# Fourteen instead of ten of the FFN's pairs computed by seven products of halves

## The chip, the cores and the metric

The kernel runs on one core of a Trainium2 chip: TensorE (PE) multiplies matrices, with its weight loads shown apart as PEld; VectorE (DVE), ScalarE (ACT) and GpSimd (POOL) do the rest; SyncE (SP) issues most DMAs. The metric is the device time of one execution in microseconds; the median of three runs before the change is 1286.7 us (1284.71 to 1290.56).

## The reference

A decoder trunk of two layers on 512 tokens of width 1024, in float32. Layer 0 mixes tokens with an RG-LRU block, layer 1 with RWKV-7; behind each stands the same gated FFN with a short convolution, which the change concerns:

```python
D_MODEL = 1024; SEQ = 512; D_FF = 3 * D_MODEL; FFN_CONV = 3

def _conv_ffn(x, norm, w_up, conv_w, conv_b, w_down):
    h = _rmsnorm(x, norm)
    u = jnp.einsum('btd,df->btf', h, w_up)
    gate = _causal_dwconv(u[..., :D_FF], conv_w, conv_b)
    hid = jax.nn.gelu(gate, approximate=True) * u[..., D_FF:]
    return jnp.einsum('btf,fd->btd', hid, w_down)
```

## The kernel before

Precision. Every float32 operand is split into a hi part (rounded, by ScalarE) and a lo part (the rest, by VectorE), and a product is three matmuls: hi x hi, hi x lo, lo x hi (mm3, lines 47 to 54). Each matmul has its own weight load.

The FFN. The 3072 gate columns and the 3072 up columns are cut into twelve *pairs* of 256 gate and 256 up columns (n = 0 to 11). Two pairs and the part of the down projection that has become ready make one period: the loop at the end of ffn runs the products of two pairs, up to product 7 of the odd one, and then down, inside which the odd pair's products 3 and 4 are put after the first piece of the first 512 columns.

A *whole* pair (class Whole) has four products G0, U0, G1, U1: 256 columns of gate or up, the upper or lower 512 of the 1024 inner rows, all 512 tokens. Each is 24 matmuls of 128x512 into banks accG and accU of PSUM, and has one weight of 512 KB to load and split (lines 94 and 97).

A *halves* pair (class Halves) sees gate and up as two column blocks, the inner rows as two halves and the tokens as two halves, and computes the eight products of such 2x2 blocks by seven, in the manner of Strassen and Winograd. Each is 24 matmuls of 128x256, named by number; they run in the order 1, 5, 6, 2, 7 and then 3, 4. They write three banks: A (products 1, 6, 7, 4 one on top of the other), F (5, then 3 on top) and D (2). Between products on one bank what stands there is read: ScalarE copies bank A after 1, 6 and 7 into a tile s (line 769), and VectorE adds bank F to the copy made after 7 (line 775), so that product 4 has to wait for that copy and product 3 for that addition. The token-side operands (sums of the input's halves) are made once for each layer.

A halves pair's weights are sums of blocks. Five tiles of 512 KB are loaded on SP's queue (line 166); to two of them (for products 5 and 7) an accumulating DMA from POOL's queue adds a second block as it loads (line 168). Product 6's weight is product 1's plus product 5's (VectorE, line 741), product 3's is product 6's plus one more block (an accumulating DMA, line 752, after 6's split). All seven are split (lines 747 and 748).

What sets the order. The tile framework schedules each engine's instructions from the program's order and its own estimates; each engine then takes its list in order. Weights are made two products ahead (ahead), loads of a halves pair start at G0 of the whole pair before it. All raw, hi and lo weight tiles of the kernel share one ring of 21 buffers of 4 KB a partition ("b4"): a load waits until the buffer it gets has been read for the last time.

Of the kernel before, what the change touches and what calls it, by code (L numbers as in the profile page):

```python
# [28 lines left out]
WARM2 = 20  # L29
WARM = 14  # L30

HALVES = (3, 5, 7, 9, 11)

PARAMS = [
    [("lru_b_in", 16), ("lru_conv_w", 32), ("lru_conv_b", 8),
# [9 lines left out]
class Kernel:  # L45
# [54 lines left out]
    def plan_weights(self):  # L100
# [4 lines left out]
        def piece(w, r0, c0, k):  # L105
            return w[r0 : r0 + k * P, c0 : c0 + D // k].rearrange("(k p) c -> p k c", p=P)
# [9 lines left out]
        def ffn(l):  # L116
            up, dn = I["ffn_w_up"][l], I["ffn_w_down"][l]

            def gu(six):


                for n in range(2 * six, 2 * six + 2):
                    self.quads.append(len(plan))
                    a = lambda i, j: piece(up, j * 512, (1 - i) * DFF + n * 256, 4)
                    if n in HALVES:
                        for first, more in (((0, 0), None), ((1, 1), (1, 0)), ((0, 1), None), ((1, 0), (0, 0)), ((1, 1), None)):
# [461 lines left out]
    def ffn(self, l, xs, finish, after=None):  # L588
        nc, tc = self.nc, self.tc
        last = l == 1  # L590
        with tc.tile_pool(name=f"ffn{l}", bufs=1) as pool:
# [21 lines left out]
            def start(c):  # L613
                if c == 0:
                    norm.append(self.norm_end(rbs))
                    next(norm[0])
                elif c == 1:
                    next(norm[0])
                    if last:
                        self.push(by_tokens())  # L620
# [14 lines left out]
            def operands():  # L635
                n1, t2, t3, t4 = sums

                def parts(t, k, f):
                    nc.scalar.copy(t[:, 0, k], f)
                    nc.vector.tensor_tensor(t[:, 1, k], f, t[:, 0, k].bitcast(F32), ALU.subtract)  # L640

                stt = nc.vector.scalar_tensor_tensor
                minus = pool.tile([P, 4], F32, name="minus")
                nc.vector.tensor_scalar(minus, self.vec("ffn_norm", l * 8 + 4, 4), -1.0, None, ALU.mult)
                for k in range(4):
                    x1, x2 = self.x[:, k, :], self.x[:, 4 + k, :]
                    d, f = two(t("s", 7)), two(t("s", 7))
                    nc.scalar.mul(d[:, 0], x1[:, H:], gain(k))
                    stt(d[:, 1], x1[:, 0:H], gain(k), d[:, 0], ALU.mult, ALU.subtract)
                    parts(n1, k, d[:, 1])  # L650
                    stt(f[:, 0], x2[:, H:], minus[:, k : k + 1], d[:, 1], ALU.mult, ALU.subtract)
                    parts(t2, k, f[:, 0])
                    stt(f[:, 1], x2[:, 0:H], minus[:, k : k + 1], f[:, 0], ALU.mult, ALU.subtract)
                    parts(t4, k, f[:, 1])
                    stt(d[:, 1], x2[:, H:], gain(4 + k), d[:, 0], ALU.mult, ALU.subtract)
                    parts(t3, k, d[:, 1])
                op = {i: [tuple(part[:, h] for part in xs[k + k0][:2]) for k in range(4)]
                      for i, k0, h in ((1, 0, slice(0, H)), (2, 4, slice(0, H)), (3, 4, slice(H, T)))}
                for i, v in ((5, n1), (6, t2), (7, t3), (4, t4)):
                    op[i] = [(v[:, 0, k], v[:, 1, k]) for k in range(4)]  # L660
                return op
# [133 lines left out]
            pairs, hids = {}, []  # L795
            kind = lambda n: Halves if n in HALVES else Whole
            seq = [(n, p) for n in range(12) for part in kind(n).order for p in part]
            made, at = [0], [0]

            def ahead(j):  # L800
                while made[0] < min(j, len(seq)):
                    n, p = seq[made[0]]
                    if n not in pairs:
                        pairs[n] = kind(n)(n)
                    pairs[n].weights(p)
                    made[0] += 1

            def products(upto, more=2):

                while True:  # L810
                    n, p = seq[at[0]]
                    at[0] += 1
                    ahead(at[0] + more)
                    pairs[n].product(p)
                    if p == "G0" and n + 1 in HALVES:
                        self.weights_load(quads[n + 1] + 4)
                    if n == 0 and p in ("G0", "U0"):
                        start(int(p == "U0"))
                    if n == 1 and p == "U0":
                        op.update(operands())  # L820
                    if p == 7:
                        self.weights_split(behind[n] + 2)
                    if (n, p) == upto:
                        return
# [57 lines left out]
            for n in range(3, 12, 2):  # L882
                products((n, 7))
                if n == 11 and not last:
                    self.norm_begin()
                    self.push(self.lora_weights())
                down(n, 2 * n - 6, 4 if n < 11 else 8, lambda: products((n, 4)), lambda: ahead(at[0] + 2))
# [898 lines left out]
```

## Time and profile before

| what | us |
|---|---|
| median of three runs | 1286.7 |
| the profiled execution | 1286.57 |
| its span, from the first to the last instruction | 1284.5 |
| the first FFN's period with pairs 6 and 7, busy TensorE | 63.0 of 63.0 |
| the same of the second FFN | 63.1 of 63.1 |

Times within the trace count from the start of the span. A row of a timeline gives start, duration, engine, line, operation, result and operands, and, in brackets, how long the engine had been idle before it and what released it. A group's row gives count and shortest, median and longest duration. For DMAs "to landing" is from issue to the data's arrival.

### The profile page before, as it was taken

Reading aid. Unit: us, or ns where it says so; the run is one execution under the profiler, and the core shown is the slowest. Engines: PE = TensorE matmul, PEld = TensorE weight load, DVE = VectorE, ACT = ScalarE, POOL = GpSimd, SP = SyncE. Lnnn points to the kernel's source line nnn. Section 1 sums busy time; section 2 is a strip of 40 time slices with the busy share of each in tenths; the row PEclk is TensorE's granted clock in tenths of the full one; section 3 lists DMA queues with packets and bytes.
Section 4 is the critical chain, followed back from the end, with each engine's and each line's share of the span. In section 5 each row is a group of like instructions: output and inputs, shape, how many; then the busy total and the mean of one; then the engine's idle time right before and its main releaser. Section 6 shows DMA issues by size and latency. Waiting matters only on the chain. (4 is left out here: it accounts for less than half of the span.)

```text
span 1284.5 us, 22413 instructions
## 1 busy us (share of the span) xinstructions
PE 1260.1 (98%) x9259; PEld 1069.9 (83%) x9259; DVE 928.6 (72%) x1412; ACT 643.5 (50%) x1006; POOL 134.1 (10%) x206
## 2 busy tenths in 40 slices
PE   9999999999999999999999999999999999999998
PEld 8777888989898989877678888778889898989896
DVE  5998678767676767788899867778866666666654
ACT  6697455434343343468745346545644343443442
POOL 3000001010100000010002144420010101000000
PEclk9999999999999999999799999999999999999999
DMA  7312335545454544422113122132355454545431
GB/s 220 113 52 97 98 120 111 164 99 177 86 180 83 180 96 122 148 66 79 66 48 92 52 62 81 48 100 77 110 110 163 100 177 86 181 82 181 95 136 65
DMA packets 117829, 141.37 MB, mean 110 GB/s; under 512 B 10138, under 2 KB 91748, under 8 KB 117600
## 3 DMA queue, kind: packets, MB, share of 16 engines
q1 hardware_dynamic: 100528, 122.44, 29.6%
q0 software_dynamic: 16624, 16.47, 8.3%
q8 instruction: 72, 1.18, 0.4%
q10 hardware_dynamic: 576, 1.05, 0.2%
q14 instruction: 29, 0.24, 0.1%
HBM read 135.41 MB, written 4.52 MB: 109 GB/s over the span
## 5 line engine op out<-in xcount | busy, mean ns | idle before, releaser
L97 DVE TENSOR_TENSOR wl<-raw,wh 128x1024 fp32r<-128x1024 f32 (+1 forms) x161 | 194.5, 1213 | 123.8 <-ACT wh L94 104.0
L94 ACT CAST wh<-raw 128x1024 fp32r<-128x1024 f32 (+1 forms) x161 | 166.0, 1043 | 181.6 <-PE acc L54 45.8
L54 PE MATMUL accU<-xs,wh 128*128 128x512 f32 x448 | 138.6, 391 | 0.0
L54 PE MATMUL accG<-xs,wh 128*128 128x512 f32 x448 | 138.6, 390 | 0.0
L54 PE MATMUL acc<-hid,wh 128*128 128x512 f32 x384 | 117.9, 389 | 0.0
L748 DVE TENSOR_TENSOR lo<-raw,hi 128x1024 fp32r<-128x1024 f32 x70 | 85.4, 1222 | 39.4 <-PE accU L54 32.0
L747 ACT CAST hi<-raw 128x1024 fp32r<-128x1024 f32 x70 | 73.6, 1053 | 60.4 <-PE accU L54 25.3
L54 PEld LDWEIGHTS accG<-xs,wh 128*128 128x128 f32 x448 | 83.7, 188 | 17.1
L54 PEld LDWEIGHTS accU<-xs,wh 128*128 128x128 f32 x448 | 83.6, 188 | 17.1
L54 PE MATMUL accU<-xs,wl 128*128 128x512 f32 x224 | 87.2, 389 | 0.0
L54 PE MATMUL accG<-xs,wl 128*128 128x512 f32 x224 | 87.2, 389 | 0.0
L54 PE MATMUL accA<-xt,hi 128*128 128x256 f32 x480 | 83.5, 277 | 0.0
L54 PEld LDWEIGHTS acc<-hid,wh 128*128 128x128 f32 x384 | 71.4, 188 | 14.3
L54 PE MATMUL acc<-xs,wh 128*128 128x512 f32 x256 | 80.9, 398 | 0.0
L694 DVE SCALAR_TENSOR_TENSOR cv<-gpad,pv,cv 128x512 f32<-128x512 f32 x96 | 69.1, 748 | 13.1 <-ACT cv L692 12.7
L848 PE MATMUL acc<-wh,hid 128*128 128x512 f32 (+1 forms) x200 | 76.2, 381 | 0.0
L849 PE MATMUL acc<-wl,hid 128*128 128x512 f32 (+1 forms) x200 | 76.1, 381 | 0.0
L847 PE MATMUL acc<-wh,hid 128*128 128x512 f32 (+1 forms) x200 | 76.1, 381 | 0.0
L168 POOL DMA_DIRECT2D raw<-in_ffn_w_up_dram x20 | 25.7, 1286 | 474.1 <-DVE x L863 166.2
L54 PE MATMUL acc<-hid,wl 128*128 128x512 f32 x192 | 74.3, 389 | 0.0
L54 PEld LDWEIGHTS accA<-xt,hi 128*128 128x128 f32 x480 | 72.6, 188 | 0.0
L54 PE MATMUL accA<-xt,lo 128*128 128x256 f32 x240 | 66.3, 276 | 0.0
(411 smaller groups left out, 2947.3 us busy)
## 6 DMA issues: line engine op xcount, KB each, us to landing
raw<-in_ffn_w_up_dram SPq DMA_DIRECT2D x106, 512.0 KB, 3.6
raw<-in_ffn_w_down_dram SPq DMA_DIRECT2D x48, 512.0 KB, 3.8
raw<-in_ffn_w_up_dram POOLq DMA_DIRECT2D x30, 512.0 KB, 5.7
raw<-in_rwkv_w_rkv_dram SPq DMA_DIRECT2D x24, 512.0 KB, 3.6
raw<-in_lru_w_in_dram SPq DMA_DIRECT2D x16, 512.0 KB, 4.0
raw<-in_lru_w_out_dram SPq DMA_DIRECT2D x8, 512.0 KB, 3.8
raw<-in_rwkv_w_out_dram SPq DMA_DIRECT2D x8, 512.0 KB, 3.4
xd<-x SPq DMA_DIRECT2D x8, 256.0 KB, 2.1
```

The source lines that it names most:

```text
L54: mm = lambda *a, **kw: self.nc.tensor.matmul(ps, *a, skip_group_check=more, **kw)
L94: put = (self.nc.vector.tensor_copy if dve else self.nc.scalar.copy)(hi, src)
L97: self.nc.vector.tensor_tensor(lo, src, hi.bitcast(F32), ALU.subtract)
L168: self.nc.gpsimd.dma_start(raw, more, accum_op=ALU.add)
L694: nc.vector.scalar_tensor_tensor(cv, pair.gp[:, e, j : j + T], cw(j), cv, ALU.mult, ALU.add)
L747: nc.scalar.copy(hi, f[p])
L748: tt(lo, f[p], hi.bitcast(F32), ALU.subtract)
L847: nc.tensor.matmul(ps, hh[:, s], wh[:, k, m], start=kk == 0, stop=False)
L848: nc.tensor.matmul(ps, hl[:, s], wh[:, k, m], start=False, stop=False)
L849: nc.tensor.matmul(ps, hh[:, s], wl[:, k, m], start=False, stop=kk == blocks - 1)
```

## The change

Pairs 6 and 10 join the list of those that are computed by halves; each period from n = 6, 7 and from n = 10, 11 then has two halves pairs in a row. The hooks are moved to fit: the loads of an odd halves pair behind an even halves pair are called for at product 6 of that even pair, and the next weights are split at product 7 of odd pairs only.

```diff
-HALVES = (3, 5, 7, 9, 11)
+HALVES = (3, 5, 6, 7, 9, 10, 11)
...
                     pairs[n].product(p)
-                    if p == "G0" and n + 1 in HALVES:
+                    if p in ("G0", 6) and n % 2 == 0 and n + 1 in HALVES:
                         self.weights_load(quads[n + 1] + 4)
...
-                    if p == 7:
+                    if p == 7 and n % 2:
                         self.weights_split(behind[n] + 2)
```

In the rows below, raw58 to raw62 are the loaded weights of pair 6, raw63 to raw67 those of pair 7 (in order of products 1, 5, 2, 7, 4); hi and lo carry the number of the product, accA_2934 and accF_2965 are banks of pair 6, accA_3178 is bank A of pair 7, wh and wl are the split weights of the down projection.

TensorE in the first FFN, before: the end of product 7 of pair 7, and the piece of the down projection that follows.

```order
L54 MATMUL accA_3082<-xt_1485,hi7_3140 128x256 x2
L54 MATMUL accA_3082<-xt_1485,lo7_3141 128x256
L54 MATMUL acc0_3245<-hid_2525,wh67_3235 128x512 x2
L54 MATMUL acc0_3245<-hid_2525,wl67_3236 128x512
L54 MATMUL acc0_3245<-hid_2525,wh67_3235 128x512 x2
```

And now, behind product 7 of pair 6: the last of the six matmuls of pair 7's product 1, nine of pair 6's product 4, and the first of its product 3.

```order
L54 MATMUL accA_3178<-xs1_1279,hi1_3095 128x256 x2
L54 MATMUL accA_3178<-xs1_1279,lo1_3096 128x256
L54 MATMUL accA_2934<-xt_1486,hi4_3063 128x256 x2
L54 MATMUL accA_2934<-xt_1486,lo4_3064 128x256
L54 MATMUL accA_2934<-xt_1486,hi4_3063 128x256 x2
L54 MATMUL accA_2934<-xt_1486,lo4_3064 128x256
L54 MATMUL accA_2934<-xt_1486,hi4_3063 128x256 x2
L54 MATMUL accA_2934<-xt_1486,lo4_3064 128x256
L54 MATMUL accF_2965<-xs4_1412,hi3_3032 128x256 x2
```

Where a piece of 24 down matmuls of 128x512 lay between products 7 and 4, there are six matmuls of 128x256 now.

ScalarE at the same place, before: its copies after products 1, 6 and 7 of pair 7, with casts of down weights between them.

```order
L769 COPY s_3107<-accA_3082 128x512
L747 CAST hi4_3201<-raw66_3138 128x1024
L769 COPY s_3168<-accA_3082 128x512
L94 CAST wh67_3235<-raw67_3233 128x1024
L94 CAST wh68_3241<-raw68_3239 128x1024
L769 COPY s_3229<-accA_3082 128x512
```

And now the copies of pair 6.

```order
L769 COPY s_2959<-accA_2934 128x512
L747 CAST hi3_3032<-raw58_2749 128x1024
L769 COPY s_3020<-accA_2934 128x512
L747 CAST hi4_3063<-raw62_2990 128x1024
L747 CAST hi1_3095<-raw63_3022 128x1024
L747 CAST hi5_3125<-raw64_3024 128x1024
L769 COPY s_3091<-accA_2934 128x512
```

The casts of pair 7's first two weights, of which raw64 is one that an accumulating DMA adds to, stand ahead of the copy after product 7.

VectorE at the end of pair 5, before: from the gate's rows to the first sum of the down projection.

```order
L782 SCALAR_TENSOR_TENSOR gpad1_1480<-accA_2554,rb_1565 128x2x256
L97 TENSOR_TENSOR wl59_2921<-raw59_2860,wh59_2920 128x1024
L694 SCALAR_TENSOR_TENSOR cv_2799<-gpad1_1480,pv_79,cv_2799 128x512
L694 SCALAR_TENSOR_TENSOR cv_2804<-gpad1_1480,pv_79,cv_2804 128x512
L694 SCALAR_TENSOR_TENSOR cv_2799<-gpad1_1480,pv_79,cv_2799 128x512
L694 SCALAR_TENSOR_TENSOR cv_2804<-gpad1_1480,pv_79,cv_2804 128x512
L863 TENSOR_TENSOR x_68<-x_68,acc0_2717 128x512
```

And now.

```order
L741 TENSOR_TENSOR raw58_2749<-raw59_2751,raw58_2749 128x1024
L748 TENSOR_TENSOR lo5_2790<-raw59_2751,hi5_2789 128x1024
L694 SCALAR_TENSOR_TENSOR cv_2819<-gpad1_1480,pv_79,cv_2819 128x512
L694 SCALAR_TENSOR_TENSOR cv_2824<-gpad1_1480,pv_79,cv_2824 128x512
L694 SCALAR_TENSOR_TENSOR cv_2819<-gpad1_1480,pv_79,cv_2819 128x512
L694 SCALAR_TENSOR_TENSOR cv_2824<-gpad1_1480,pv_79,cv_2824 128x512
L97 TENSOR_TENSOR wl56_2837<-raw56_2721,wh56_2836 128x1024
L863 TENSOR_TENSOR x_68<-x_68,acc0_2717 128x512
```

Pair 6's sum and split have come ahead of the convolution, and the lo part of the third down weight, which was made earlier, has come behind it. The lo part of the fourth (wl57) has moved behind the eight sums and products that follow.

## The prediction

> **What bounds the kernel now.** The page comes first, then the busy time by stretches of the second FFN, then the chain of waits there.
>
> ```profile
> span 1284.5 us, 22413 instructions
> PE 1260.1 (98%) x9259; PEld 1069.9 (83%) x9259; DVE 928.6 (72%) x1412; ACT 643.5 (50%) x1006; POOL 134.1 (10%) x206
> ...
> core 0: us, PE busy (x) PEld busy (x) DVE busy (x) ACT busy (x) POOL busy (x), PEclk, DMA share, GB/s
> 374.90:437.90 63.00, 63.00 (x361) 55.50 (x361) 41.70 (x51) 24.98 (x31) 3.81 (x3) 1.00 0.50 133
> 1066.90:1129.99 63.09, 63.09 (x362) 55.58 (x361) 39.87 (x48) 25.27 (x30) 3.85 (x3) 1.00 0.50 134
> ```
>
> A stretch of 63 us is one period: a whole pair, a halves pair and their share of the down projection, in layer 0 (first row) and layer 1 (second). TensorE is busy in all of it and the clock is 1.00, so only matmul time can be taken away there. VectorE has 41.7 of 63.0 us, ScalarE 25, the DMA engines half. The chain of one period in layer 1:
>
> ```profile
> 1066.90 5.44 PE accG L54 x24
> 1072.34 5.44 PE accU L54 x24
> 1077.78 5.44 PE accG L54 x24
> 1083.22 5.44 PE accU L54 x24
> 1088.66 2.87 PE accA L54 x24
> 1091.53 2.74 PE accF L54 x24
> 1094.27 2.72 PE accA L54 x24
> 1096.99 2.86 PE accD L54 x24
> 1099.85 2.74 PE accA L54 x24
> ...
> 1108.05 2.87 PE accF L54 x24
> 1110.92 2.74 PE accA L54 x24
> ...
> 1129.99 5.44 PE accG L54 x24
> ```
>
> The columns are start, duration, what. A whole pair is four products of 24 matmuls, 4 x 5.44 = 21.76 us. A halves pair is seven products (in order 1, 5, 6, 2, 7 and, after a piece of the down projection, 3 and 4): 2.87 + 2.74 + 2.72 + 2.86 + 2.74 + 2.87 + 2.74 = 19.54 us. The rest of the 63.09 is 21.79 us of down projection.
>
> **The change part by part.** Pairs 6 and 10 turn from whole to halves in both layers: four times 21.76 - 19.54 = 2.22 us of matmuls go, 8.9 us. Nothing more can be won: TensorE has no idle time in these stretches that could vanish too.
>
> At one place a rule of the Trainium skill speaks against this. TensorE: Matmul & The Clock Gate, section Back-to-back issue gap, says that in a stream of weight loads and matmuls the spacing is set by both, and gives 131 ns a matmul at 512 columns and 81 at 128. By those figures a whole pair's 96 matmuls would take 12.6 us and a halves pair's 168 at least 13.6, a loss. The trace disagrees: 24 matmuls of 512 columns take 5.44 us, 227 ns each, and 24 of 256 take 2.72 to 2.87, 113 to 120 each.
>
> What the other engines get, per changed pair:
>
> ```profile
> 376.76 2.73 DVE L694 SCALAR_TENSOR_TENSOR cv<-gpad,pv,cv 128x512 f32<-128x512 f32 x4
> 379.42 1.28 DVE L863 TENSOR_TENSOR x<-x,acc 128x512 f32<-128x512 f32 x2
> 380.61 1.29 DVE L787 TENSOR_TENSOR s<-s,ge 128x512 f32<-128x512 f32 x2
> 382.42 1.29 DVE L789 TENSOR_TENSOR hid<-s,hid 128x512 fp32r<-128x512 f32 x2
> 394.18 1.23 DVE L741 TENSOR_TENSOR raw<-raw,raw 128x1024 f32<-128x1024 f32 x1
> 402.08 2.55 DVE L748 TENSOR_TENSOR lo<-raw,hi 128x1024 fp32r<-128x1024 f32 x2 [3.20 <-PE accU L54]
> 364.58 0.69 DVE L775 TENSOR_TENSOR s<-s,accF 128x512 f32<-128x512 f32 x1 [0.46 <-ACT s L769]
> ```
>
> VectorE: a whole pair has four weight splits of 1.2 us, eight operations of 0.68 and the convolution's 2.7, some 13 us. A halves pair has seven splits and an addition (8 x 1.23 = 9.8), seven of 0.69 (4.8), the convolution (2.7) and lines 787 and 789 (2.6), 19.9 us. That is 7 us more: 48.6 of a period of 60.9, 80%. ScalarE goes from 25 to 30 us (three more casts of 1.05 us, three copies of 0.59). Both stay below TensorE, so their work costs nothing on average; what can cost is its place in a queue. DMA: eight transfers of 512 KB for four (five on SP's queue, three accumulating on POOL's), from 8.4 to 10.5 MB a period, a share of about 0.65.
>
> Three places have little room. I count from t = 0 at 374.9, when the last matmul of the halves pair before the changed one ends, with operations back to back on VectorE at the spacing of the rows (0.60 for 128x512, 0.66 for line 694, 1.13 for 128x1024).
>
> *First, the down weights.* TensorE does the second piece of the first down columns (24 x 0.227 = 5.4), then seven matmuls that need no lo part, and wants the third piece's lo at 7.0. VectorE has the gate (0.1 to 0.7), the new line 741 and the new split (to 3.0), the convolution (to 5.65), then that lo: ready at 6.9. The fourth lo is wanted at 13.2, after 25 more down matmuls and four of product 1; VectorE adds eight operations of 0.60 and has it at 12.8. So 0.1 and 0.4 us are left; I count 0.2 us of waiting, between 0 and 0.8 (half of one more 1.13 operation at each).
>
> *Second, and the main term, the accumulated weight of the next pair.* So far the 21.76 us of a whole pair lay between two halves pairs, time in which the next one's weights came in. Now pair 7's loads reuse buffers that pair 6 still reads: by the waits in the program, its first weight waits for the split of pair 6's product 7, its second (the one that a second DMA adds to) for the end of product 1. The other two loads stand behind these on SP's queue. Product 1 ends at 19.2 (all down matmuls 16.3 + 2.87); VectorE ends that split at about 19.0, so the second load goes out at 19.4, one of three in a row.
>
> ```profile
> 424.65 0.88 SPq L166 DMA_DIRECT2D raw<-in_ffn_w_down_dram  x2
> DMA to landing us min/median/max: 3.7/4.1/4.6
> ...
> DMA to landing us min/median/max: 3.6/4.1/5.2
> ...
> L168 POOL DMA_DIRECT2D raw<-in_ffn_w_up_dram x20: 1258/1276/1378, 195.1 to 1195.4; - x20
> ...
> DMA to landing us min/median/max: 5.6/5.7/7.6
> ```
>
> The first two lines are a burst of two loads of 512 KB (3.7 and 4.6), the third four loads within 6.6 us, the last the accumulating loads. So: 19.4 + 4.6 = 24.0, POOL issues the accumulation, + 5.7 = 29.8. (Behind it on POOL stands only the one for product 7 of pair 7, wanted 14 us later or more.) ScalarE takes its instructions in order, and the cast of this weight now stands ahead of the copy of bank A after pair 6's product 7:
>
> ```profile
> 391.36 1.05 ACT L747 CAST hi<-raw 128x1024 fp32r<-128x1024 f32 x1 [0.30 <-PE acc L54]
> 363.96 0.59 ACT L769 COPY s<-accA 128x512 f32<-128x512 f32 x1 [1.10 <-PE accA L54]
> ```
>
> Cast to 30.8, copy to 31.4, and TensorE goes on at 31.5. It had finished product 7 at 30.2 (19.2 + 2.74 + 2.72 + 2.86 + 2.74) and six matmuls of pair 7's product 1 at 31.0, and stands before product 4, which may not write bank A until the copy is done: 0.5 us of waiting. Each us that the accumulation is later is a us more; 1 us earlier and there is none. With the longest rows (5.2 and 7.6) it is 3.0. I take the likelier rows: 0.5.
>
> *Third*, product 3 wants line 775, which VectorE does after the new line 741 on the same weight: 741 ends at 31.4, 775 at 32.1, and product 3 begins at 31.5 + 1.0 (nine matmuls; fifteen in layer 1) = 32.5. It hides behind the second wait.
>
> The order is the same at pairs 6 and 10 of both layers, so each saves 2.22 - 0.7 = about 1.5: 6.1 us in all. The profiled execution took 1286.57 us (its span and 2.1 around it), the median is 1286.7: forecast 1286.6 - 6.1 = **1280.5 us**.
>
> **The rivals.** *All hidden.* With loads that land in 3.7 and 5.7 us the cast is over before the copy is due, and 1286.6 - 8.9 = 1277.7 follows. For it: the lengths are the common ones. Against: three loads leave in a row, and the first two waits leave 0.1 and 0.4 us.
>
> *The wait eats the saving.* Two us more at each place (accumulations beside other loads, as they now are): 2.7 us of waiting each, and 1286.6 + 4 x 0.5 = 1288.6. For it: the 7.6 in the row, 1.9 above the median. Against: that one is rare.
>
> *Slower.* One mechanism, the same chain (load, accumulation, cast, copy, product 4), beside twice as many accumulations: with the longest landing of a plain load in layer 1,
>
> ```profile
> DMA to landing us min/median/max: 3.3/3.7/6.8
> ```
>
> 6.8 and 7.6 give 2.2 + 1.9 more, 4.8 us a place: 1286.6 + 4 x 2.6 = 1297. It decides from a chain that is 1.5 us longer than I count.
>
> *Weight loads set the pace.*
>
> ```profile
> L54 PEld LDWEIGHTS accA<-xt,hi 128*128 128x128 f32 x480 | 72.6, 188 | 0.0
> ```
>
> If 188 ns a load could not overlap, a halves pair would take 168 x 0.188 = 31.6 us, 9.8 more than a whole one, and the time would be 1326; it decides from 21.76 / 168 = 130 ns a matmul. The halves pairs that run already show 113 to 120. The Trainium skill's rule above is this rival.
>
> **How the numbers follow.** All hidden (under 0.3 us a place) 0.25; the forecast (0.3 to 1.4) 0.47; the wait eats the saving (1.4 to 3.8) 0.20; slower 0.07; weight loads 0.01. A measurement of this kernel can tell about 0.5%, 6.4 us, from no change: faster means below 1280.3. All of the first case is there and 0.17 of the second, 0.42; slower is the last two, 0.08; within 0.5% has the other 0.50. The range, 1277.0 to 1288.6, goes from the first case less 0.7 of scatter to the third's price, and leaves out the slower cases and the longest waits of the third.
>
> **What would show it.** Right: a period of about 61.5 us with pair 6 or 10 in it, seven products of 2.7 to 2.9 us, and one short wait of TensorE before product 4 of the even pair, released by ScalarE's copy, with an accumulating load behind it. Wrong: periods of 60.9 with no gap (all hidden); gaps over 2.2 us (saving eaten); gaps at the lo parts of the down weights instead (VectorE short of time); products longer than 3 us; or a difference outside the FFN.

## The result, and the profile after

The changed kernel takes 1303.57 us (median of four runs, 1301.74 to 1307.06), the kernel before in the same comparison 1285.7 us (1283.18 to 1290.56): a ratio of 1.0147, 95% interval 1.0113 to 1.0182. It is slower by 1.5%, and the interval is clear of 1. The forecast was 1280.5 us with a range up to 1288.6.

The head of the page of after (the profiled execution took 1307.06 us):

```profile
span 1305.3 us, 23093 instructions
PE 1261.0 (97%) x9547; PEld 1081.4 (83%) x9547; DVE 952.7 (73%) x1440; ACT 658.4 (50%) x1030; POOL 149.2 (11%) x218
```

TensorE's busy time has not fallen by 8.9 us, and the span has grown by 20.8 us. The wait view of TensorE shows the first half of the reason (two FFNs, apart by the "..."; columns: us in total, times, longest):

```profile
PE accA L54 <- ACT s L769: 5.3, 2, 3.2
PE acc L54 <- ACT wh L94: 3.0, 2, 1.7
PE acc L54 <- DVE wl L97: 1.7, 2, 0.9
...
PE accA L54 <- ACT s L769: 6.6, 2, 3.4
PE acc L847 <- ACT wh L94: 3.7, 2, 1.9
PE acc L849 <- DVE wl L97: 0.9, 1, 0.9
```

Before, this view was empty in the stretches with pairs 6 to 11. Now there are 21.2 us: 9.3 at the down weights (the prediction's first place) and 11.9 at the copies of bank A (its second). The second half of the reason stands in stretches of 2 to 7 us around pairs 6 and 7 of layer 0 (columns as in the prediction; the clock, the DMA share and GB/s are the last three):

```profile
304.00:309.00 5.00, 5.00 (x34) 4.61 (x33) 0.00 (x0) 1.05 (x1) 0.00 (x0) 1.00 0.99 328
322.00:328.00 6.00, 6.00 (x30) 5.04 (x29) 6.00 (x10) 3.01 (x4) 0.00 (x0) 1.00 0.01 3
334.00:341.00 7.00, 7.00 (x63) 7.00 (x63) 1.22 (x1) 3.04 (x4) 0.42 (x1) 1.00 1.12 321
...
348.00:350.00 2.00, 2.00 (x11) 2.00 (x12) 2.00 (x3) 0.79 (x1) 0.00 (x0) 0.61 0.30 47
350.00:352.00 2.00, 2.00 (x12) 2.00 (x11) 1.44 (x2) 0.00 (x0) 0.26 (x1) 0.54 0.00 0
```

Two things are to be seen. The DMA engines are full at 304 to 309 and at 334 to 341 us and idle at 322 to 328 between: the loads come in bursts. And at 348 us the clock drops to about half for some 3.4 us. The chain of waits tells what happened there (start, duration, what):

```profile
301.34 7.51 DMA raw<-in_ffn_w_up_dram
...
309.41 5.91 DMA raw<-in_ffn_w_up_dram
...
334.37 5.67 DMA raw<-in_ffn_w_up_dram
...
340.57 5.67 DMA raw<-in_ffn_w_up_dram
...
347.90 1.89 PE accA L54 x9
349.79 3.83 PE accF L54 x24
```

The first two rows are the load and the accumulation of pair 6's second weight, the next two those of pair 7's. Where before the chain was TensorE alone, it now goes through these transfers. The last two rows are the slow clock: 9 matmuls in 1.89 us instead of 1.02, 24 in 3.83 instead of 2.87, 1.8 us together. The two FFNs have five such stretches: one behind each of the four waits for a copy and one behind the down weights' waits in layer 1. The queues in which the late weights stand, on ScalarE:

```profile
315.40 1.05 ACT L747 CAST hi<-raw 128x1024 fp32r<-128x1024 f32 x1 [6.88 <-DMA raw<-in_ffn_w_up_dram]
316.36 1.52 ACT L692 ACTIVATE cv<-gpad,pv 128x512 f32<-128x512 f32 x2
317.78 1.03 ACT L94 CAST wh<-raw 128x1024 fp32r<-128x1024 f32 x1
...
346.32 1.04 ACT L747 CAST hi<-raw 128x1024 fp32r<-128x1024 f32 x1 [2.92 <-DMA raw<-in_ffn_w_up_dram]
347.27 0.58 ACT L769 COPY s<-accA 128x512 f32<-128x512 f32 x1
```

and on VectorE:

```profile
315.42 1.23 DVE L741 TENSOR_TENSOR raw<-raw,raw 128x1024 f32<-128x1024 f32 x1 [2.66 <-DMA raw<-in_ffn_w_up_dram]
```

At the first place both engines stand before pair 6's second weight until 315.4, with the down weights' cast (line 94 at 317.78) behind it. At the second ScalarE stands 2.92 us before pair 7's second weight, with the copy behind it.

By stages: from its first G0 matmul to RWKV's first matmul, the first FFN went from 368.1 to 379.7 us; from there to the second FFN's first G0 matmul the RWKV stage went from 366.7 to 362.4; the second FFN, to the end, from 393.2 to 406.6. In the FFNs: 7.4 saved (by e5's periods, below), 21.2 of waits, 0.6 of waits for hid (the FFN's gated hidden rows) at the end of the first FFN, five times about 1.8 for the clock, 23.4 in all, of the 25.0 measured; 1.6 are not traced. Of the RWKV stage's 4.3 some 3.4 go with its clock, which was at half for 13.7 us in the profiled execution of before and for 6.8 in that of after; the change does not touch this stage. The profiled execution of after is the slowest of its four, with a mean granted clock of 0.989 against 0.991 to 0.992, so the count of five is that of this execution.

### The profile page after: what moved, and what is told of

Same layout as the page of the kernel before. It is cut to its first block, busy times and chain, and to the rows that moved or that the text cites. A ratio compares the mean times of both kernels' runs of the same rounds, so it can differ in the third digit from the quotient of the medians.

```text
span 1305.3 us, 23093 instructions
## 1 busy us (share of the span) xinstructions
PE 1261.0 (97%) x9547; PEld 1081.4 (83%) x9547; DVE 952.7 (73%) x1440; ACT 658.4 (50%) x1030; POOL 149.2 (11%) x218
## 4 chain that ended last, share of the span: by engine, by line
PE 71%; DVE 13%; DMA 8%; ACT 4%; issue 2%; POOL 0%; SPq 0%; POOLq 0%; ACTq 0%; DVEq 0%
PE acc L54 19%; PE accA L54 9%; PE accU L54 8%; PE accG L54 8%; DMA raw<-in_ffn_w_up_dram 8%; PE accF L54 5%; PE acc L849 3%; PE acc L847 3%; PE acc L848 3%; PE accD L54 2%; DVE wl L97 2%; DVE X L1309 1%; PE acc L1255 1%; DVE mt L970 1%; PE s L1423 1%
## 5 line engine op out<-in xcount | busy, mean ns | idle before, releaser
L747 ACT CAST hi<-raw 128x1024 fp32r<-128x1024 f32 x98 | 103.1, 1052 | 163.4 <-DMA raw<-in_ffn_w_up_dram 55.6
L748 DVE TENSOR_TENSOR lo<-raw,hi 128x1024 fp32r<-128x1024 f32 x98 | 119.0, 1221 | 49.8 <-PE accA L54 22.2
L54 PE MATMUL accA<-xt,hi 128*128 128x256 f32 x672 | 120.5, 282 | 11.9 <-ACT s L769 11.9
L54 PEld LDWEIGHTS accA<-xt,hi 128*128 128x128 f32 x672 | 103.9, 192 | 12.7 <-ACT s L769 12.7
L54 PE MATMUL accU<-xs,wh 128*128 128x512 f32 x320 | 99.2, 391 | 0.0
L54 PE MATMUL accG<-xs,wh 128*128 128x512 f32 x320 | 99.2, 391 | 0.0
L54 PE MATMUL accA<-xt,lo 128*128 128x256 f32 x336 | 94.4, 281 | 0.0
L54 PEld LDWEIGHTS accG<-xs,wh 128*128 128x128 f32 x320 | 59.6, 188 | 12.1
L54 PEld LDWEIGHTS accA<-xt,lo 128*128 128x128 f32 x336 | 64.7, 193 | 0.0
L54 PE MATMUL accU<-xs,wl 128*128 128x512 f32 x160 | 62.3, 390 | 0.0
```

Source lines behind the costliest of these rows:

```text
L54: mm = lambda *a, **kw: self.nc.tensor.matmul(ps, *a, skip_group_check=more, **kw)
L747: nc.scalar.copy(hi, f[p])
L748: tt(lo, f[p], hi.bitcast(F32), ALU.subtract)
```

## The experiments

The kernel before was run beside each. "Waits" are sums of TensorE's wait view over the two FFNs as above; the two-pair period runs from G0 of pair 4 to G0 of pair 8 and was 126.2 us before in both layers.

**Which accumulated weight.** e1, e2 and e5 leave out the accumulation to product 5's weight in pairs 7 and 11, in 6 and 10, or in all four. All matmuls, casts and additions of the engines are done, with incomplete weights.

```diff
-... ((1, 1), (1, 0)), ...
+... ((1, 1), None if n in (7, 11) else (1, 0)), ...
```

> Left out: the block that an accumulating DMA adds to the weight of product 5 of pairs 7 and 11 (2 DMAs a layer). Theory (the four waits before product 4 of pairs 6 and 10, 11.9 us, come from this accumulation, whose cast ScalarE has ahead of the copy of bank A; the half clock behind each of them, 3.4 us long and so 1.7 us, is their consequence): these waits fall below 1 us in all, the clock stays at 1.00 there, time 1303.6 - 11.9 - 4 x 1.7 = about 1285. Rival, VectorE is short of time (its work stays as it is): waits of the same sum in another place, time above 1297. Rival, the clock dips by itself (more weight loads, not the waits): only the 11.9 go, the four half-clock stretches stay, time about 1292.

> Left out: the block that an accumulating DMA adds to the weight of product 5 of pairs 6 and 10. Theory (at the border from pair 5 to 6 and from 9 to 10 ScalarE holds the cast of this weight ahead of the gate and of the down weights' casts, and VectorE the sum of line 741): the 8.8 us of waits for casts of down weights and the 4.6 us for their lo parts go to under 3 us in all, the waits before product 4 (11.9 us) stay: time about 1303.6 - 11 = 1292 to 1293. Rival, VectorE is short of time: at least half of the 13.4 us stays, time above 1297.

> Left out: the added block of product 5's weight in pairs 6, 7, 10 and 11, the two omissions of the first two experiments together. Theory (two waits at each place, independent of each other, both from an accumulating load ahead of other work in ScalarE's queue): the waits are gone, 8.9 us of matmuls are saved, time 1284.7 - 8.9 = 1276 to 1278. Rival (what is left of the waits, 8.5 us in the first experiment, is VectorE's lack of time and only moves): at least 5 us of waits in the FFNs, time 1281 or more.

e1: 1286.33 us, ratio 1.0014 (0.9999 to 1.0030); of the waits at the copies 1.4 us is left, those at the first place are 7.1 (9.3 in after), and there is no stretch of half clock in the FFNs. e2: 1288.99 us, 1.0043 (1.0026 to 1.0060); the down weights' waits are gone, the copies' are 11.4. e5: 1277.55 us, 0.9949 (0.9931 to 0.9967), periods of 124.33 us in both layers. TensorE's waits in e5 are no more than

```profile
PE acc L54 <- DVE hid L789: 0.4, 1, 0.4
PE acc L54 <- ACT hid L788: 0.2, 1, 0.2
...
PE accA L54 <- ACT s L769: 1.3, 1, 1.3
```

So most of the saving is there (1.9 us a period, where 2.22 were forecast), VectorE and ScalarE with all of their added work are not short of time, and with the accumulations the waits of both places go. Leaving out an accumulation also takes 512 KB out of a burst of transfers, so these three runs do not tell the late weight from the load on the DMA engines; the runs from e4 on leave nothing out. Without the one the kernel gains 17.2 us on after (e1), without the other 14.6 (e2), without both 26.0: the two gains overlap, though e5 expected them to be independent.

**One of the two pairs.** e3 takes pair 10 back out of the list: HALVES = (3, 5, 6, 7, 9, 11).

> Pair 6 by halves, pair 10 whole, in both layers (12 pairs of 24). Theory (a loss of the same size at each of the four places, 17.9 / 4 = 4.5 us): half of the loss, time 1285.7 + 9 = about 1294.7, two waits before product 4 instead of four. Rival, the time goes lost elsewhere (the end of a layer, the RWKV stage with another order): nearer to 1285.7 or to 1303.6 than to the middle.

1292.76 us, 1.0057 (1.0030 to 1.0084), with waits of 6.6 and 5.7 us, all at pairs 6 and 7. With one place in each layer instead of two, about 0.4 of after's loss (0.57 of 1.47 per cent) is left: the loss goes by places.

**The place in the queue.** e4 puts the copy of bank A ahead of the odd pair's cast, and line 775 ahead of its line 741:

```diff
+ with tc.issue_after(pairs[pair.n - 1].add.ins):      # pairs 7, 11
      tt(f[1], f[5], f[1], ALU.add)
...
+ with tc.issue_after(pairs[pair.n - 1].put.ins):      # product 5 of pairs 7, 11
      nc.scalar.copy(hi, f[p])
```

> All 14 pairs, nothing left out; only the order of two instructions on ScalarE and of two on VectorE: the cast of pair 7's (11's) second weight is held behind the copy of bank A after pair 6's (10's) product 7, the sum of line 741 behind line 775. Theory (it is the place in the queue that makes the late transfer cost TensorE's time): the 11.9 us before product 4 go, and the half clock behind them, time about 1285, though the transfers land as late as before. Rival, the transfers are too late in any order (TensorE then waits for pair 7's product 5 instead): waits of 8 us or more before products 5 or 6 of pairs 7 and 11, time above 1297.

1293.66 us, 1.0081 (1.0052 to 1.0110): half of the expected gain. The copies' waits fall from 11.9 to 4.9 and the clock stays full, but 7.9 us of waits are left at other places (0.6 of them for hid, as in after), and those for lo parts of down weights have grown from 2.6 us (three) to 6.0 (eight). What the late weight holds up moves down the queue. In e4's chain of waits the next late one is pair 7's last accumulated weight, that of product 3 (line 752, which is 756 in e4), for which ScalarE's next cast waits until 357.56. POOL's row of it, and the chain's:

```profile
351.24 1.27 POOL L756 DMA_DIRECT2D raw<-in_ffn_w_up_dram  x1 [7.58 <-DVE lo L752]
...
351.24 6.24 DMA raw<-in_ffn_w_up_dram
```

**The order of products and loads.** e6 runs 1, 2, 5, 6, 7 in pairs 6, 7, 10 and 11, so that the accumulated weight is wanted one product later; e7 also holds line 741 behind line 775; e8 keeps the order and loads product 5's weight ahead of product 1's.

```diff
+ late = ((1, 2, 5, 6, 7), (3, 4))
...
+ order = lambda n: Halves.late if {n ^ 1, n} <= set(HALVES) else kind(n).order
```

> Nothing left out. In pairs 6, 7, 10 and 11 the products run in the order 1, 2, 5, 6, 7 instead of 1, 5, 6, 2, 7, so the weight with the accumulation is wanted one product (2.8 us) later and its cast stands behind the gate, the down weights' casts and the copy of bank A. Theory (place in the queue, and room of a few us): the casts' waits go at both places; VectorE still has line 741 (waits for the accumulation) ahead of line 775 (which product 3 waits for), so some 1 to 3 us a place stay: time 1280 to 1287, no half clock but where a wait of over 1 us is left. Rival (the transfers are too late in any order, as the fourth experiment's waits for other weights suggest): time above 1290.

> The same, with line 741 of pairs 7 and 11 held behind line 775 on VectorE. Theory: the wait of product 3 goes too, under 3 us of waits in the FFNs, time 1277 to 1281, faster than before. Rival (the transfers are too late in any order): product 5 or 6 of pairs 7 and 11 waits instead, time as in the kernel sent with it.

> The changed kernel with one difference: in pairs 6, 7, 10 and 11 the load of product 5's weight stands ahead of that of product 1's on SP's queue. Theory (the load is late because it is the third to fifth of a burst on DMA engines that are full, 7.5 us instead of 4): it lands 1.5 to 3.5 us earlier, the accumulation with it; each of the eight waits is 1 to 3 us shorter, time 1290 to 1297. Rival (the load is late only because its buffer comes free late): it lands as late as before, time 1301 or more.

e6: 1311.89 us, 1.0228 (1.0203 to 1.0253), a miss. The down weights' waits at the first place are gone, but there are 16.2 us at line 776 before bank F and 7.6 more before bank A. The load of pair 7's second weight, which takes a buffer that pair 6 frees, is now released by the end of product 2 (it leaves at 333.24; in after it left at 334.37, behind product 1), and its accumulation took 7.11 us: the release moved along with the product. e7: 1313.61 us, 1.0240 (1.0214 to 1.0266), the same wait at the copies instead (21.9 us). e8: 1295.85 us, 1.0097 (1.0073 to 1.0122), as expected: the place in the burst is worth some 8 us.

**Where the loads are called for.** e9 changes one number of after:

```diff
-                    if p in ("G0", 6) and n % 2 == 0 and n + 1 in HALVES:
+                    if p in ("G0", 1) and n % 2 == 0 and n + 1 in HALVES:
```

> One edit: the loads of the odd halves pairs 7 and 11 are called for behind the even pair's product 1 instead of behind its product 6. By the dependencies of the program the second weight's plain load of pair 7 then takes a buffer that the third down weight frees, about 6.5 us earlier; TensorE's order stays. Theory (the second place is late because its load is called for late): the copies' waits of 11.9 us in the changed kernel go below 4 us, the half clock behind them goes, the first place stays: 1286 to 1293 us, the two-pair periods at 126 to 128.5. Rival (the DMA engines are full in that stretch, so an earlier call only moves the burst and makes the first place later): no gain, 1300 to 1306 us, with the weights' waits at the first place longer than the changed kernel's.

1289.26 us, 1.0041 (1.0026 to 1.0055): 14.3 us of the loss are gone. The waits of e9:

```profile
PE acc L54 <- ACT wh L94: 2.4, 2, 1.7
PE acc L54 <- DVE wl L97: 1.7, 2, 0.9
PE accA L54 <- ACT s L769: 0.7, 1, 0.7
...
PE acc L847 <- ACT wh L94: 2.2, 2, 1.1
PE acc L849 <- DVE wl L97: 1.7, 2, 0.9
PE accA L54 <- ACT s L769: 1.4, 1, 1.4
```

The copies' 11.9 us are 2.1, the first place's are 8.0, and neither FFN has half clock. The accumulation of pair 7's second weight leaves 4.1 us earlier (that of pair 6's only 0.5), in after

```profile
340.57 1.27 POOL L168 DMA_DIRECT2D raw<-in_ffn_w_up_dram  x1 [10.37 <-DMA raw<-in_ffn_w_up_dram]
```

and in e9

```profile
336.46 1.27 POOL L168 DMA_DIRECT2D raw<-in_ffn_w_up_dram  x1 [7.05 <-PE accF L54]
```

e10 and e11 join this with the edits of e6 and e4:

> The same early call, with product 2 ahead of product 5 in the pairs 6, 7, 10 and 11 (the order that lost in e6 and was late there by its call). Theory: both places then have their second weight in time; 1277 to 1284 us, waits below 4 us in all. Rival (too late in any order, because the load and the accumulation of two pairs don't fit between the down block and the product): waits of over 10 us and 1292 us or more.

> The early call of e9, with the copy of bank A and line 775 ahead of the odd pair's cast and line 741 as in e4. Theory: e4 left 12.8 us of waits because pair 7's later loads came late behind its late second weight; with the early call these go, and only the first place stays: 1282 to 1289 us. Rival (the first place's burst is the larger part and makes all of it late): within 2 us of e4's 1293.7.

e10: 1313.56 us, 1.0228 (1.0212 to 1.0243), the rival's numbers (waits of 24.9 us, 21.1 of them before a cast of line 747, which is line 748 there). e11: 1292.57 us, 1.0058 (1.0037 to 1.0079), the rival's time too. The copies' waits are 2.0 us, against 2.1 in e9, so there was little left to win there; those for lo parts of down weights are 6.1, as e4's 6.0 were, against 3.4 in e9. That the held cast costs this is inferred, not tested. What e10's ScalarE stood before was understood only with the next runs.

**The first place.** e12 is e9 with the third and fourth down weight's casts put ahead of pair 6's (and 10's) second weight:

```diff
+                    if p == 4 and n in (5, 9):
+                        self.weights_split(behind[n] + 4)
                     ahead(at[0] + more)
```

> The early call of e9, and the casts and subtractions of the third and fourth down weight (lines 94 and 97) put ahead of pair 6's and 10's second weight on ScalarE and VectorE, with line 741 of these pairs falling behind the down block's evictions. All products, loads and accumulations of the changed kernel stay. Theory (the first place is a queue behind a late weight; the weight itself has over 10 us left until its product): the 8.0 us of waits for wh and wl that e9 kept go, waits of at most 3 us are left, 1278 to 1284 us, ratio below 1.000. Rival (what e9 lost at the first place is only passed on, because pair 6's second weight or pair 7's loads then come late further down, or VectorE is short of time there): waits of 6 us or more in other rows and 1287 us or more.

1296.36 us, 1.0098 (1.0077 to 1.0119): worse than e9. The first place is as expected (1.6 us of its 8.0 are left), but 13.1 us stand at the copies. I took that for pair 7's own weight, and put its load first in its burst, in e9 (e13) and in e12 (e14), by another order in the plan of loads: pair 7's second and first weight, pair 6's last, then the others.

> e9 with one more edit: of the loads that leave at the down block's end, that of pair 7's (11's) second weight goes first, then that of its first weight, and pair 6's last weight, which is needed latest, goes third instead of first. Theory (the second place is decided by when this one load lands, and in e9 it stood third in a burst): the copies' last 2.1 us of waits go, the first place's 8 us stay: 1284 to 1289 us. Rival (the burst as a whole sets the landing, so that the order within it does nothing): 1289 to 1293 us with the copies' waits unchanged or larger.

> e12 (down weights' casts first, no wait left in the first place, but 13.1 us of waits at the copies) with the same edit. Theory: e12's load of pair 7's second weight took 9.1 us to land as the third of the burst; as the first it lands in 4 to 6 us, so the copies' waits fall from 13.1 us to below 4: 1279 to 1286 us. Rival (load, accumulation and cast don't fit between the down block's end and the copy in any order): waits of over 8 us at the copies and 1290 us or more, so that what e9 gained at the second place was only bought by its waits at the first.

e13: 1287.44 us, 1.0024 (1.0007 to 1.0041), which can't be told from e9; of the copies' waits, which were to go, 1.4 us are left. e14: 1295.25 us, 1.0080 (1.0065 to 1.0095), with 12.0 us at the copies. So it was not the burst's order. ScalarE's and POOL's rows of e12 name another accumulation:

```profile
333.40 1.06 ACT L747 CAST hi<-raw 128x1024 fp32r<-128x1024 f32 x1 [1.20 <-PE accF L54]
339.36 1.04 ACT L747 CAST hi<-raw 128x1024 fp32r<-128x1024 f32 x1 [4.91 <-DMA raw<-in_ffn_w_up_dram]
340.31 0.58 ACT L769 COPY s<-accA 128x512 f32<-128x512 f32 x1
...
327.97 1.27 POOL L752 DMA_DIRECT2D raw<-in_ffn_w_up_dram  x1 [15.80 <-DVE lo L748]
```

The cast at 339.36 is that of pair 6's product 3, whose weight is made by line 752's accumulation. VectorE had begun line 741, from which it follows, only at 324.05, behind the convolution and the down projection's sums. The accumulation left at 327.97, as the burst began, and took until 339.3. In e10 the same transfer left at 333.20 and landed at 341.37. e15 is e12 with products made three ahead instead of two at that one point, so that line 741 comes earlier; e16 has e14's order of loads too.

```diff
-                    ahead(at[0] + more)
+                    ahead(at[0] + (3 if p == 4 and n in (5, 9) else more))
```

> e12 with line 741 and the casts of product 6 in pairs 6 and 10 called for one product earlier, at product 4 of the pair before. In e12 and e14 line 741 came only 12.6 us after the down block's start (324.05 and 323.86 us), so that the accumulation of line 752, which it releases, left at 327.97 us, into the burst, and the cast that waits for it held the copies. Here line 741 stands right ahead of the fourth down weight's subtraction. Theory: the accumulation of line 752 leaves at about 320 us, where the DMA engines are nearly idle (share 0.05 to 0.10 in e12), no copy waits for it, waits of at most 4 us in all are left: 1279 to 1286 us. Rival (pair 7's own load and accumulation after the down block's end are late in any case): copies' waits of over 8 us and 1290 us or more.

> e15 with the load order of e13 and e14 (pair 7's second weight first in the burst). Theory: whatever copy waits e15 keeps because of pair 7's own weight go as well: 1278 to 1284 us, not above e15. Rival as in e15.

e15: 1282.87 us, 0.9989 (0.9976 to 1.0002). e16: 1281.85 us, 0.9981 (0.9970 to 0.9993). In e15 the accumulation leaves at 321.44, while little else moves (windows and POOL's rows of e15; compare 0.01 at 322 to 328 in after):

```profile
322.00:328.00 6.00, 6.00 (x32) 5.10 (x31) 6.00 (x11) 2.33 (x4) 0.72 (x1) 1.00 0.74 131
328.00:334.00 6.00, 6.00 (x55) 6.00 (x54) 2.24 (x3) 2.59 (x3) 0.26 (x1) 1.00 1.01 342
...
321.44 1.27 POOL L752 DMA_DIRECT2D raw<-in_ffn_w_up_dram  x1 [9.76 <-DVE lo L748]
```

The waits of e15 are 5.3 us (at most 4 were expected), with 0.6 for hid. Those of e16, where line 769 has become 784, are 4.6, and the clock stays full in both FFNs:

```profile
PE acc L54 <- DVE wl L97: 1.6, 2, 0.8
PE accA L54 <- ACT s L784: 1.2, 1, 1.2
PE acc L54 <- DVE hid L804: 0.3, 1, 0.3
PE acc L54 <- ACT hid L803: 0.2, 1, 0.2
...
PE accA L54 <- ACT s L784: 1.3, 1, 1.3
```

e16 does all the products, loads and accumulations of the changed kernel, in another order: 21.7 us less by the medians, and 2.8 us less than the kernel before. Its interval lies below 1, but the gain is under the 0.5% that count here as a difference, and e5, without the four accumulations, was lower still at 1277.55. e15 and e16 can't be told apart. Whether line 741's earlier place would do without the down casts ahead, and on after without e9's call, was not tried.

## Why the prediction was wrong

*A stretch misread, without effect.* The first FFN's stretch from 374.90 on, which the table ahead and the prediction take for pairs 6 and 7, is that of pairs 8 and 9. Pairs 6 and 7 lie one period earlier, from 311.86 to 374.90, and TensorE is busy there for 63.04 of 63.04 us, so the sums stand.

*The saving: right in kind, a sixth too large.* e5 keeps all instructions of TensorE, VectorE and ScalarE and is 7.1 us below before; a period is 1.9 us shorter instead of 2.22, and where the rest goes is not traced. VectorE was busy for 82% of the changed period in layer 0 and 70% in layer 1 (80% was forecast), and weight loads set no pace.

*First place: the step that failed.* It went through VectorE's queue from t = 0 on with "the new line 741 and the new split (to 3.0)" and counted 0.2 us a place. That took pair 6's second weight as there. It landed at 315.32, 3.5 us after t = 0 (311.86 in after), since its load, one of three that left within 1 us behind loads of down weights, took 7.51 us, and the accumulation 5.91. The landings that the forecast used were of thinner bursts, at most 5.2. With slacks of 0.1 and 0.4 us the 3.5 us became 9.3 us of waiting in four places, 2.3 each. 6.7 of these were for casts of ScalarE, whose queue the prediction did not follow at this place, and 2.6 for VectorE's lo parts. That the late weight is behind it is shown twice: without its accumulation (e2) the down weights' waits are zero, and with nothing left out and the casts of the third and fourth down weight put ahead of it (e12) they are 1.6 us, where e9 has 8.0.

*Second place: the mechanism right, the size wrong.* The chain (load, accumulation, cast, copy, TensorE) is what ScalarE's rows show, and e1 takes the waits from 11.9 to 1.4 us. Counted from the end of product 1 (about 334.1 us, where the copy after it begins), the load took 5.67 us instead of 4.6 (6.4 to 6.9 at the other three places), POOL needed 0.5 us to issue, which I had left out, and the accumulation took 5.67 against 5.7: the 0.5 us of waiting became 2.0 there and 3.2 to 3.4 in the other three places. That lies between the rival "the wait eats the saving" (2.7 a place) and the rival "slower" (4.8). The third place hid behind the second as forecast: no wait in after is for line 775.

*Left out: the clock.* The prediction took it as 1.00. Behind five of the waits it was at half for some 3.4 us, about 1.8 us more a time, 9 in all.

*The sum.* Four places at 0.7 us of waiting were 2.8; measured were 21.2 (9.3 instead of 0.8 at the first places, 11.9 instead of 2.0 at the second), and 9 for the clock. The rival "slower" reached 1297 from the second place alone; no rival had both places at once, and none the clock.

*What would show it.* Gaps at the down weights and gaps over 2.2 us were named as signs against it, and both came, those at the down weights not because VectorE was short of time, as the sign had it.

## What to carry to other kernels

Before a slack is counted on an engine's queue, follow each operand back to its DMA, in the burst it leaves in and from the buffer it waits for: here 0.2 us counted as VectorE's was a weight 3.5 us late. When a change packs weight traffic more densely, look for the stretches between bursts in which the DMA engines are idle and move what can be released there: with the order of calls and queues alone, and no work removed, 21.7 us came back here. A stalled instruction at the head of a queue is mended by what feeds it, and after each repair the next wait in the same queue has to be named anew.

## What the runs showed of the hardware

The clock: in after each wait of TensorE before bank A (2.0 to 3.4 us) was followed by some 3.4 us at half clock (0.61 and 0.54 in the windows above), which made the one of 2.0 us cost 3.9. The length of the wait alone does not decide. In after a wait of 1.78 us (to 1197.97) had half clock behind it and one of 1.94 us (to 1065.43) had none. In the other runs one of 1.38 us (e8, to 319.24) had it, while one of 2.93 us (e2, to 346.37) and one of 3.01 us (e12, to 1085.57) had none. All waits above 3.1 us in the FFNs had it. What else decides is not shown here.

Transfers in a burst: from issue to landing the accumulating ones took 5.5 to 8.2 us in after, but 11.3 in e12 for the one that left at 327.97, into a burst. The three plain loads of 512 KB that left within 1 us at 301 us in after took 6.5 to 8.3 us, at 281 to 328 GB/s.
